# Five transformed pairs instead of four in each quarter of the down projection, with sums of weights brought in by transfers into the residual's room

## The chip, the cores and the metric

The kernel runs on one core of one Trainium2 chip. The metric is the time of one execution on the device, in microseconds (us), as the median of several runs. Engines go by the profile's names: PE is the matrix engine (PEld its weight loads), DVE the vector engine, ACT the scalar engine, POOL and SP the two engines whose queues issue transfers here. Each engine works through its own instructions strictly in the program's order.

## The reference

One layer of a decoder trunk on 256 tokens of width D = 2048, in fp32: a block of attention in two branches, then a channel mixer, then a gated embedding. The change lies in the channel mixer and in what keeps the residual `h` from it to the end:

```python
    h = h + rmsnorm(mix, g_mix_post[i])
    u = rmsnorm(h, g_ffn_pre[i])
    up = causal_depthwise_conv(u @ w_up[i], conv_w[i], conv_b[i])
    gate_ff, value = jnp.split(up, [D_FF], axis=-1)
    f = (jax.nn.gelu(gate_ff, approximate=True) * value) @ w_down[i]
    h = h + rmsnorm(f, g_ffn_post[i])
    e = p[i] @ w_ple_in[i]
    h = h + jax.nn.sigmoid((h @ w_ple_gate[i]).astype(jnp.float32)).astype(h.dtype) * e
```

D_FF is 5632, so `w_up` has 2 x 44 columns of tiles of 128 and `w_down` 44 rows of tiles.

## The kernel before

**Weights in two parts.** All weights lie packed in DRAM in the order in which PE uses them. An item is eight 128x128 blocks, one 128x1024 tile of 512 KB. `load` (L199) brings an item into one of 5 raw tiles (NRAW), `high` (L228) lets ACT write its rounded high part `hi`, and `low` (L291) lets DVE write the remainder `lo` = raw - hi (L301). There are 7 pairs of hi and lo tiles (NSPL). A product is three matmuls, high times high, low times high, high times low (`three_wide`, L943, matmuls on L945; in `up`, `mul` with L382 and L384).

**What sets the order.** The order is written out by hand through `tick` (L326), which runs each time PE begins a new item: it lets ACT write high parts up to six items ahead of PE (`reach`, L220), lets DVE write the low parts of all items up to five ahead, and then runs the deferred work that is due (`defer`, `due`). `lows` (L317) also emits the load of an item as soon as a raw tile is released in the program's order, on SP's queue. So DVE's queue holds, at each tick, first the low parts for items that PE will need later, and then the deferred vector work.

**Quarters.** The channel mixer runs in four quarters, q = 0 to 3 (loop at L1382): 22 column groups of `up` (16 blocks each), whose evacuation (`up_evac`, L1211) leaves 11 rows of tiles in `ft`, then `down` for these 11 rows. `down` of a quarter has three parts: a group of output columns 0 to 1023 (`strassen`, L1253), and two groups of 512 columns, `plain(2)` and `plain(3)` (L1393, `four`). In q = 0 `plain(2)` comes ahead of `strassen`, in the other quarters directly behind it.

**Pairs.** In `strassen`, rows go in pairs (DROWS = 8, four pairs) and the last three rows singly (`plains`, 12 matmuls each). A pair takes seven products, 21 matmuls of 512 columns, where two single rows take 24. For that it needs sums of activations, which `parts` (L1193) makes during `up` into the tile `mixed` (four subtractions, one copy by ACT, one subtraction), and sums of weights. A pair is four items of the stream: the first raw item, two items of sums, and half an item. The sums are `raw` tiles of their own (`weight_sums`, L240): for most pairs DVE makes them, four additions of 128x512 (L254, L255, L257, L258); for the first two pairs of each quarter (DSUM) the first two additions are left to transfers: `sum_early` (L280) loads the first raw item a second time into a tile `tsum` and adds half of the second item to it twice through POOL's queue (`accum_op=OP.add`, L277), so that DVE makes two (L257, L258). The two tiles of `tsum` are one of their own and two borrowed from the tag `t`.

**Banks.** Results lie in 8 PSUM banks handed out by `bank` (L415). `strassen` uses all eight: products 1, 5, 6, 7 and the four output tiles. In q > 0 `plain(2)` needs two banks again while DVE still has the outputs to put together: ACT copies product 1 away (L1279), and DVE's `join_to` (L1307) begins with `x2 = product 6 + copy of product 1` (L1311), seven more instructions (L1312 to L1318) follow, and `ends` (L1320) adds the four output tiles. The first bank of `plain(2)` is released by the copy of product 1; the second one is the bank of product 6, and is released by L1311. `join_to` is deferred: it stands in DVE's queue behind the low parts that the tick of the first single row emits. In q = 0 `join_first` (L1298) reads product 6, and the group that waits for its bank is `plain(3)`.

**The residual.** `home` (L1243) writes the residual, 16 KB a partition, into the tile `hx` early in `up`; it lies there unused until `apply` (L1443) adds the normalized output of `down` to it. Before, its room holds the first half of `e` for a moment (`turn`, L1105), which is written to DRAM and read back later (`e0`).

## Time and profile before

| | |
|---|---|
| median of 3 runs | 1434.43 us (1434.07 to 1434.95) |
| the profiled execution | 1434.18 us; its span, first to last instruction, is 1432.0 us |
| granted PE clock, mean | 0.999 |
| ACT busy | 860.0 us, 60% of the span |
| transfers on SP's queue | 285.76 MB, 59.6% of the time of 16 DMA engines |
| transfers on POOL's queue | 11.54 MB, 4.7% |

Rows of groups give the busy time and the mean duration of one instruction; rows of the timeline give start, duration, engine, line, operation and operands, and in brackets how long the engine was idle before and what ended that. Instructions overlap a little: one starts before the record of the one ahead ends, so the distance from start to start is what an instruction costs in a full queue. The chain of waits goes from the last instruction back to the first, at each step to what released it.

### The profile page before, as it was taken

What the parts mean: (1) busy time and instruction counts of PE and PEld (TensorE: products, weight loads), DVE (VectorE), ACT (ScalarE), POOL (GpSimd) and SP (SyncE); (2) the same over time, 40 slices, a digit from 0 to 9 for tenths busy, and PEclk for the clock granted to TensorE, in tenths of its full rate; (3) what the DMA queues carried; (4) which work ended last, traced back from release to release, by engine and by line L of the source; (5) the groups of instructions that cost most, each with busy time, mean ns of one, the idle gap of its engine ahead of it and who ended that gap; (6) DMA issues with size and microseconds to landing.
All of it is one profiled execution on the core that took longest, in us unless ns stands there. A gap on an engine that the chain in (4) does not pass through costs nothing.

```text
span 1432.0 us, 20556 instructions
## 1 busy us (share of the span) xinstructions
PE 1423.4 (99%) x7511; PEld 1222.8 (85%) x7511; DVE 1167.4 (82%) x1791; ACT 860.0 (60%) x1296; POOL 39.4 (3%) x49
## 2 busy tenths in 40 slices
PE   9999999999999999999999999999999999999998
PEld 8888888888888888998888888888888888888787
DVE  7876666669889965779999788987889878899797
ACT  7665555566555655576665666655665555657464
POOL 0000000002110000000000000000000000000000
PEclk9999999999999999999999999999999999999999
DMA  7754746479985766547657865377653776538654
GB/s 290 268 168 160 245 141 219 148 240 255 298 230 200 268 216 218 185 162 226 203 170 245 256 196 177 118 277 235 206 179 114 272 233 207 183 112 303 181 176 162
DMA packets 87908, 298.60 MB, mean 209 GB/s; under 512 B 9728, under 2 KB 10368, under 8 KB 87552
## 3 DMA queue, kind: packets, MB, share of 16 engines
q1 hardware_dynamic: 81472, 285.76, 59.6%
q0 software_dynamic: 6336, 11.54, 4.7%
q8 instruction: 59, 0.97, 0.3%
q14 instruction: 41, 0.34, 0.1%
HBM read 294.11 MB, written 3.15 MB: 208 GB/s over the span
## 4 chain that ended last, share of the span: by engine, by line
PE 93%; DVE 6%; ACT 1%; issue 0%; ACTq 0%; DVEq 0%
PE mm L382 32%; PE mm L945 27%; PE mm L384 16%; PE mm L708 2%; PE mm L710 2%; PE mm L709 2%; PE mm L863 2%; PE mm L864 2%; PE mm L865 2%; DVE lo L295 2%; DVE lo L301 1%; PE S L382 0%; DVE wsum L257 0%; PE mm L404 0%; PE mm L403 0%; PE mm L402 0%
## 5 line engine op out<-in xcount | busy, mean ns | idle before, releaser
L301 DVE TENSOR_TENSOR lo<-raw,hi 128x1024 fp32r<-128x1024 f32 (+1 forms) x498 | 582.0, 1186 | 105.6 <-ACT hi L238 100.7
L382 PE MATMUL mm<-u,hi 128*128 128x512 f32 x1804 | 627.4, 392 | 0.0
L238 ACT ACTIVATE hi<-raw 128x1024 fp32r<-128x1024 f32 (+1 forms) x498 | 504.5, 1027 | 175.6 <-PE mm L382 54.2
L384 PE MATMUL mm<-u,lo 128*128 128x256 f32 x1791 | 501.4, 280 | 0.0
L382 PEld LDWEIGHTS mm<-u,hi 128*128 128x128 f32 x1804 | 336.7, 187 | 72.4
L384 PEld LDWEIGHTS mm<-u,lo 128*128 128x128 f32 x1791 | 338.5, 189 | 0.7
L945 PE MATMUL mm<-hi,ft 128*128 128x512 f32 x544 | 173.8, 390 | 0.9 <-ACT hi L234 0.9
L945 PE MATMUL mm<-hi,u 128*128 128x512 f32 (+1 forms) x464 | 148.0, 389 | 0.6 <-DVE u L1486 0.5
L440 ACT ACTIVATE t<-mm 128x256 f32<-128x256 f32 x131 | 49.8, 380 | 149.1 <-PE mm L384 149.1
L945 PEld LDWEIGHTS mm<-hi,ft 128*128 128x128 f32 x544 | 102.1, 188 | 22.9 <-ACT hi L234 2.2
L945 PE MATMUL mm<-lo,ft 128*128 128x512 f32 x272 | 106.3, 391 | 0.7 <-DVE lo L295 0.7
L945 PEld LDWEIGHTS mm<-hi,u 128*128 128x128 f32 x464 | 86.4, 188 | 19.1 <-DVE u L1486 2.1
L443 DVE TENSOR_TENSOR s<-mm,t 128x256 f32<-128x256 f32 x116 | 49.0, 423 | 54.1 <-ACT t L440 54.0
L945 PE MATMUL mm<-lo,u 128*128 128x512 f32 (+1 forms) x232 | 89.6, 386 | 0.0
L382 PE MATMUL mm<-mg,hi 128*128 128x512 f32 x232 | 80.5, 392 | 0.0
L234 ACT ACTIVATE hi<-wsum 128x512 fp32r<-128x512 f32 x84 | 50.7, 629 | 49.1 <-DVE wsum L257 40.2
L384 PE MATMUL mm<-mg,lo 128*128 128x256 f32 x230 | 64.4, 280 | 0.0
L945 PEld LDWEIGHTS mm<-lo,ft 128*128 128x128 f32 x272 | 51.0, 188 | 12.6 <-DVE lo L295 2.0
L1222 ACT ACTIVATE cv<-cpad,cw 128x256 f32<-128x256 f32 x88 | 52.6, 598 | 12.1 <-DVE cpad L1217 12.0
L945 PE MATMUL mm<-hi,mixed 128*128 128x512 f32 x160 | 55.8, 390 | 0.0
L295 DVE TENSOR_TENSOR lo<-wsum,hi 128x512 fp32r<-128x512 f32 x84 | 54.6, 688 | 1.3 <-ACT hi L234 0.7
L945 PEld LDWEIGHTS mm<-lo,u 128*128 128x128 f32 x232 | 43.6, 188 | 9.0 <-DVE lo L295 0.5
(327 smaller groups left out, 1837.8 us busy)
## 6 DMA issues: line engine op xcount, KB each, us to landing
raw<-in_w SPq DMA_DIRECT2D x478, 512.0 KB, 4.0
gh<-in_w SPq DMA_DIRECT2D x12, 512.0 KB, 5.9
gh<-in_w POOLq DMA_DIRECT2D x24, 256.0 KB, 7.8
raw<-in_w SPq DMA_DIRECT2D x24, 256.0 KB, 3.4
tsum<-in_w POOLq DMA_DIRECT2D x20, 256.0 KB, 7.0
hd<-in_head SPq DMA_DIRECT2D x6, 576.0 KB, 7.4
gh<-in_gx SPq DMA_DIRECT2D x6, 512.0 KB, 4.5
tsum<-in_w SPq DMA_DIRECT2D x5, 512.0 KB, 4.5
```

The lines of the kernel that those rows point to most:

```text
L234: ACT.activation(hi[i][:, n * 512:(n + 1) * 512], x, AF.Copy)
L238: ACT.activation(hi[i][:, a:b], raw[i][:, a:b] if src is None else src, AF.Copy)
L295: DVE.tensor_tensor(lo[i][:, to], x, f(hi[i][:, to]), OP.subtract)
L301: DVE.tensor_tensor(lo[i][:, a:b], raw[i][:, a:b] if src is None else src, f(hi[i][:, a:b]), OP.subtract)
L382: PE.matmul(ps, wh, rhs, start=first, stop=last, skip_group_check=True)
L384: PE.matmul(ps[:, :T], wl, rhs[:, :T], start=False, stop=last, skip_group_check=True)
L440: ACT.activation(t1[0], ps[:, T:], AF.Copy)
L443: DVE.tensor_tensor(out, ps[:, :T], t1[0], OP.add)
L708: PE.matmul(pv[t], xh, wh, start=kt == 0, stop=False)
L709: PE.matmul(pv[t], xh, wl, start=False, stop=False)
L945: PE.matmul(ps, x[i], w[j], start=first and n == 0, stop=last and n == 2, skip_group_check=True)
L1222: ACT.activation(y, c[:, 2:], AF.Identity, scale=cw[:, n, 2:3], bias=cw[:, n, 3:4])
```

## The change

DROWS becomes 10, so `strassen` has five pairs and one single row in each quarter. All five pairs get their first sums by transfers. Their places are `tsum`, the two tiles of tag `t`, and three of the four 4 KB-wide pieces into which `hx` is cut (tags hx1 to hx3); the fourth piece (hx0) holds the transformed activations of the fifth pair. To free this room the residual is written to DRAM (`h1`, 2 MB, four transfers) after `home` has made it, and read back by four transfers in the last quarter, behind the single row of `strassen`. `e0` is written in two transfers instead of one, and `finish` makes two additions of 512 columns where it made one of 1024. The pairs of the last stage (`pg`) keep what they had.

```diff
-DROWS = 8
-DSUM = 2
+DROWS = 10
+DSUM = {"down": DROWS // 2, "pg": 2}
...
-                if g[0][0] == "pairs" and p < DSUM:
+                if g[0][0] == "pairs" and p < DSUM[g[0][1]]:
                     early_sums.append(i)
...
         i = early_sums.pop(0)
-        if n == 0:
-            sum_to(i, mps["mp"].tile([128, 1024], F32, name="tsum", tag="tsum"))
+        if n != 1:
+            sum_to(i, mps["mp"].tile([128, 1024], F32, name="tsum", tag=f"hx{n - 1}" if n else "tsum"))
             return
...
-    hx = fp.tile([128, 2, D], F32, name="hx")
+    def residual():
+        return [fp.tile([128, 2, 512], F32, name="hx", tag=f"hx{n}") for n in range(4)]
+
+    hx = residual()
...
-    nc.sync.dma_start(e0, hx[:, :, :D // 2])
+    h1 = dram.tile([128, 2, D], F32, name="h1")
+    for n in range(2):
+        nc.sync.dma_start(e0[:, :, n * 512:(n + 1) * 512], hx[n])
...
+    def mixing(ps):
+        x = keep.tile([128, PAIRS, 2, 4, H], F32R, name="mixed", tag="gh")
+        for p in range(ps):
+            mixed[p] = x[:, p] if p < PAIRS else fp.tile([128, 2, 4, H], F32R, name="mixed4", tag="hx0")
...
     sp = halves()
-    mixed = keep.tile([128, PAIRS, 2, 4, H], F32R, name="mixed", tag="gh")
+    for n in range(4):
+        nc.sync.dma_start(h1[:, :, n * 512:(n + 1) * 512], hx[n])
+    mixing(DROWS // 2)
...
+    AHEAD = (0, 1, 4, 7, 10)[:DROWS // 2]
     for q in range(NQ):
...
             at_n = n - max(len(pss), q * 2 * QT) - 2
-            0 <= at_n < DSUM and sum_early(at_n)
+            at_n in AHEAD and sum_early(AHEAD.index(at_n))
...
         next(s)
         defer((None, lambda bk=bk, o=o: ends(o, bk)))
         if end:
+            hx = residual()
+            for n in range(4):
+                nc.sync.dma_start(hx[n], h1[:, :, n * 512:(n + 1) * 512])
             squared(range(2))
...
             DVE.tensor_tensor(o, o, ee[:, t, a:b], OP.mult)
-            DVE.tensor_tensor(o, o, hx[:, t, a:b], OP.add)
+            for c in range(a, b, 512):
+                x = min(b - c, 512)
+                to = ff[:, t, c:c + x]
+                DVE.tensor_tensor(to, to, hx[c // 512][:, t, c % 512:c % 512 + x], OP.add)
             nc.sync.dma_start(out[:, t, a:b], o)
```

The changed lines stand ten to twenty lines lower in the changed kernel: `join_to` begins at L1321 instead of L1311, `join_first` is L1308.

DVE in q = 1, from the last pair to the `join`. Before, the last pair of four: four additions of weights, the low parts of its four items, then the low parts of the three single rows and of the first three items of `plain(2)`, then L1311:

```order
L254 TENSOR_TENSOR wsum<-raw 128x512
L255 TENSOR_TENSOR wsum<-raw 128x512
L301 TENSOR_TENSOR lo<-raw,hi 128x1024
L295 TENSOR_TENSOR lo<-wsum,hi 128x512 x2
L257 TENSOR_TENSOR wsum<-wsum,raw 128x512
L258 TENSOR_TENSOR wsum<-wsum,raw 128x512
L295 TENSOR_TENSOR lo<-wsum,hi 128x512 x2
L301 TENSOR_TENSOR lo<-raw,hi 128x512
L301 TENSOR_TENSOR lo<-raw,hi 128x1024 x6
L1311 TENSOR_TENSOR x_9171<-mm,x_8950 128x512
L1312 TENSOR_TENSOR ff<-ff,x_8950 128x512
```

The same place in the changed kernel, the last pair of five:

```order
L301 TENSOR_TENSOR lo<-raw,hi 128x1024
L257 TENSOR_TENSOR wsum<-tsum,raw 128x512
L258 TENSOR_TENSOR wsum<-wsum,raw 128x512
L295 TENSOR_TENSOR lo<-tsum,hi 128x512 x2
L295 TENSOR_TENSOR lo<-wsum,hi 128x512 x2
L301 TENSOR_TENSOR lo<-raw,hi 128x512
L301 TENSOR_TENSOR lo<-raw,hi 128x1024 x6
L1321 TENSOR_TENSOR x_9271<-mm,x_9006 128x512
L1322 TENSOR_TENSOR ff<-ff,x_9006 128x512
```

L254 and L255 are gone from the pair. Six low parts still stand between it and the join; they are now those of one single row and of the first five items of `plain(2)`.

PE in q = 1, the end of `strassen` and the beginning of `plain(2)`, with the engines each waits for. Before, the last two matmuls of the third single row and the first four of `plain(2)`:

```order
L945 MATMUL mm<-lo,ft 128x512
L945 MATMUL mm<-hi,ft 128x512
L945 MATMUL mm<-hi,ft 128x512 [waits Activation_49]
L945 MATMUL mm<-lo,ft 128x512 [waits DVE_49]
L945 MATMUL mm<-hi,ft 128x512
L945 MATMUL mm<-hi,ft 128x512 [waits DVE_49]
```

In the changed kernel, the last matmuls of the only single row and the first four of `plain(2)`:

```order
L945 MATMUL mm<-lo,ft 128x512
L945 MATMUL mm<-hi,ft 128x512
L945 MATMUL mm<-hi,ft 128x512 [waits PE_49]
L945 MATMUL mm<-lo,ft 128x512
L945 MATMUL mm<-hi,ft 128x512
L945 MATMUL mm<-hi,ft 128x512 [waits Activation_49]
L945 MATMUL mm<-lo,ft 128x512 [waits DVE_49]
L945 MATMUL mm<-hi,ft 128x512
L945 MATMUL mm<-hi,ft 128x512 [waits DVE_49]
```

The fourth matmul of `plain(2)` writes into the bank of product 6 and waits for the join's first instruction on DVE, in both kernels; from the last matmul of a pair to it there are now 15 matmuls, where there were 39.

SP at the end of q = 3, the changed kernel, where the residual is read back (`h_5990` is the copy in DRAM, `g_12834` the gains, `e_5989` the stored half of `e`):

```order
L204 DMA raw<-in_w 128x1024 x10
L1437 DMA g_12834<-in_gains 128x2048
L204 DMA raw<-in_w 128x1024
L1444 DMA hx<-h_5990 128x2x512 x4
L204 DMA raw<-in_w 128x1024 x11
L1484 DMA ee<-e_5989 128x2x1024
```

Before, the fourth row was not there and 14 loads of weights stood between the gains and the stored half of `e`.

## The prediction

> **What bounds the kernel now.** The page comes first, its busy times and the chain that ended last:

> ```profile
> PE 1423.4 (99%) x7511; PEld 1222.8 (85%) x7511; DVE 1167.4 (82%) x1791; ACT 860.0 (60%) x1296; POOL 39.4 (3%) x49
> PE 93%; DVE 6%; ACT 1%; issue 0%; ACTq 0%; DVEq 0%
> ```

> PE is the bound almost everywhere; the 6% of the chain that are DVE's lie in few places. So I looked for them in the chain in order of time. In q = 1 it leaves PE at 905 us and comes back at 929 us (the third and the fourth pair):

> ```profile
> 915.76 0.60 DVE wsum L254
> 916.37 0.60 DVE wsum L255
> 916.97 1.14 DVE lo L301
> 918.10 1.20 DVE lo L295 x2
> 919.31 0.61 DVE wsum L257
> ...
> 922.63 0.60 DVE wsum L254
> ...
> 928.95 40.22 PE mm L945 x176
> ```

> Two things are read here. A pair whose sums DVE makes takes DVE 922.63 - 915.76 = 6.87 us. And a matmul of this form takes PE 40.22 / 176 = 0.2285 us, so the 21 of a pair take 4.80 us: inside `strassen` DVE is the slower engine and uses up a lead that it won during `up`. PE's timeline shows what that costs at the fourth pair:

> ```profile
> 928.22 0.50 PE L945 MATMUL mm<-hi,ft 128*128 128x512 f32 x1 [0.29 <-ACT hi L234]
> 928.95 0.50 PE L945 MATMUL mm<-lo,ft 128*128 128x512 f32 x1 [0.23 <-DVE lo L295]
> ...
> 939.54 0.62 PE L945 MATMUL mm<-hi,ft 128*128 128x512 f32 x2
> ```

> The brackets understate it, since the record of a matmul (0.39 us) is longer than its distance to the next. From the one that started 0.68 us ahead of 928.22 to 928.95 lie two distances of 0.2285 us too many: the loss is 0.95 us a quarter (q = 1 to 3, about 2.85 us in all). The row at 939.54 holds the third and the fourth matmul of `plain(2)`; the fourth starts at 939.54 + 0.2285 = 939.77, and it is the one that waits for the join's first instruction. How near was that? DVE's timeline from the last low part of the fourth pair on, and ACT's for the load:

> ```profile
> 928.81 0.69 DVE L301 TENSOR_TENSOR lo<-raw,hi 128x512 fp32r<-128x512 f32 x1
> 929.67 5.91 DVE L301 TENSOR_TENSOR lo<-raw,hi 128x1024 fp32r<-128x1024 f32 x5 [0.18 <-ACT hi L238]
> 937.46 1.23 DVE L301 TENSOR_TENSOR lo<-raw,hi 128x1024 fp32r<-128x1024 f32 x1 [1.88 <-ACT hi L238]
> 938.60 0.69 DVE L1311 TENSOR_TENSOR x<-mm,x 128x512 f32<-128x512 f32 x1
> ...
> 936.37 1.06 ACT L238 ACTIVATE hi<-raw 128x1024 fp32r<-128x1024 f32 x1 [2.04 <-DMA raw<-in_w]
> ```

> L1311 ends at 939.29, **0.48 us ahead** of the matmul that needs it. It stands behind six low parts, and the sixth waits for a load that could be issued only when the first of the six had freed a raw tile. From the end of the pair (929.50) to the end of L1311 are 9.8 us. In the other quarters the same pair of rows (DVE's L1311 and PE's third and fourth matmul), for q = 2, then q = 3:

> ```profile
> 1118.11 0.69 DVE L1311 TENSOR_TENSOR x<-mm,x 128x512 f32<-128x512 f32 x1
> 1119.98 0.61 PE L945 MATMUL mm<-hi,ft 128*128 128x512 f32 x2
> 1299.00 0.68 DVE L1311 TENSOR_TENSOR x<-mm,x 128x512 f32<-128x512 f32 x1
> 1300.41 0.61 PE L945 MATMUL mm<-hi,ft 128*128 128x512 f32 x2
> ```

> There the slack is 1120.21 - 1118.80 = 1.41 and 1300.64 - 1299.68 = 0.96 us. That is all the room the change has at this place.

> **The change part by part.** *PE's work.* A fifth pair saves 24 - 21 = 3 matmuls, 0.69 us a quarter, 2.74 us in four. If nothing else stood in the way, the 0.95 us of waiting at the fourth pair would go too, and `plain(2)` would reach its fourth matmul 0.95 + 0.69 = 1.64 us sooner: at 938.13 in q = 1, 1118.57 in q = 2, 1299.00 in q = 3.

> *DVE's work ahead of the join.* A pair whose sums come by transfer costs DVE no L254 and L255, and what it costs is seen in the rows of the second pair in q = 1:

> ```profile
> 905.81 0.42 DVE L443 TENSOR_TENSOR s<-mm,t 128x256 f32<-128x256 f32 x1 [1.05 <-ACT t L440]
> ...
> 908.82 0.68 DVE L257 TENSOR_TENSOR wsum<-tsum,raw 128x512 f32<-128x512 f32 x1
> 909.53 0.69 DVE L258 TENSOR_TENSOR wsum<-wsum,raw 128x512 f32<-128x512 f32 x1
> 910.15 1.28 DVE L295 TENSOR_TENSOR lo<-tsum,hi 128x512 fp32r<-128x512 f32 x2
> ...
> L1199 DVE TENSOR_TENSOR y<-cv,cv x16: 283/286/291, 662.8 to 1243.9; 128x128 f32<-128x128 f32 x16
> ```

> From start to start: L257 0.71, L258 0.62; and as in the chain's rows the first item 1.14, two low parts 1.20, two more 1.20, half an item 0.61 like any 128x512 operation there; together 5.5 us. The third and the fourth pair thus become 6.87 - 5.5 = 1.37 us shorter each, and a fifth of 5.5 us is added. Its activations add four subtractions of 0.28 us (last row), which fit into the 1.05 us that DVE stands idle ahead of 905.81, where they come in the order, and one subtraction of 128x512 (0.60 us), behind which DVE has no idle time until 929. DVE comes to the end of the last pair later by 5.5 - 2.74 + 0.6 = **3.4 us** (3.2 if L254's 0.60 and L255's 0.61 alone had to go and the rest ran tighter, 4.5 if the four subtractions found no room). Behind it stand again six low parts of 1.14 us and the same load, issued when the first of the six is done, so the stretch to L1321 (before: L1311) stays as measured.

> *The new wait.* L1321 ends at 939.29 + 3.4 = 942.7, 1122.2 and 1303.1 us, and PE starts 0.06 us later (928.89, the end of the low part, to 928.95 above). PE is there at 938.13, 1118.57 and 1299.00: **it waits 4.6, 3.7 and 4.2 us**. Against before the fourth matmul of `plain(2)` starts later by 942.75 - 939.77 = 3.0, by 2.05 and by 2.5 us, 7.55 in all. Behind it in PE's queue lies everything that is left; PE works without a pause to the next quarter, so nothing gives it back. The wait swallows both gains in these three quarters.

> *q = 0.* Here `plain(2)` comes first, DVE starts `strassen` with its full lead, and the join's first instruction is L1298:

> ```profile
> 769.84 0.69 DVE L1298 TENSOR_TENSOR ff<-mm,ff 128x512 f32<-128x512 f32 x1
> 774.02 0.62 PE L945 MATMUL mm<-hi,ft 128*128 128x512 f32 x2
> ```

> Slack 774.25 - 770.53 = 3.72 us. DVE comes 5.5 - 2.74 = 2.76 us later, PE 0.69 us sooner, and 0.27 us are left: gain 0.69, with 0.6 more on DVE a wait of 0.3.

> *Transfers.* Three more pairs a quarter load 0.5 MB more each and add 2 x 256 KB, the residual goes out (2 MB) and comes back (2 MB).

> ```profile
> raw<-in_w SPq DMA_DIRECT2D x478, 512.0 KB, 4.0
> tsum<-in_w POOLq DMA_DIRECT2D x20, 256.0 KB, 7.0
> e<-hx SPq DMA_DIRECT2D x1, 1024.0 KB, 6.3
> ee<-e SPq DMA_DIRECT2D x1, 1024.0 KB, 7.5
> ```

> The last sums are asked for nine groups of `up` before the pairs, some 50 us (16 x 0.348 = 5.57 us a group, from the rows of `up` in PE's timeline), and take 4 + 2 x 7 = 18: no cost; without that cover DVE waits at L257. The writes take SP's queue about 13 us at 6.3 us a MB. Queued behind them on SP are loads of `up`, of which five raw tiles at 2.8 us are in hand, 14 us: no cost, at worst a few us. The reads stand on SP behind loads up to the item that the join waits behind, not ahead of it; `apply` needs them at the end of `plain(3)`, some 30 us on, and they take 4 x 4 to 2 x 7.5 us. Loads of `plain(2)` queue behind them, with ten items of 2.74 us (five raw tiles, five pairs of hi and lo) in hand. Two more additions in `finish` lie under the last group's matmuls. All taken as zero; bounds 0 to +4 us together.

> *The sum*, on the profiled execution: 1434.18 + 7.55 - 0.69 = 1441.04; that execution was 0.25 us under the median of the runs, which is nothing here. I say **1441.0 us**, 0.47% slower.

> [...] In the window from 927 to 930, with 0.95 us lost, the granted clock was full:

> ```profile
> 927.00:930.00 3.00, 2.49 (x11) 1.49 (x10) 2.76 (x5) 2.99 (x5) 0.00 (x0) 1.00 0.53 178
> ```

> No stall of before lasts longer, so its trace can't tell what one of 4 us does. [...]

> **The rivals.** (1) *Faster:* the join is in time and PE stays the bound. Then both gains stand: 1434.18 - 2.74 - 2.85 = 1428.6. For it speaks that PE is 99% busy; against it that DVE would have to reach L1321 some 4 us sooner than its rows add up to. It decides at 938.1 us in q = 1. (2) *No change:* the join is late, but the sixth low part no longer waits for its load, because raw tiles are released more evenly. Its idle time was 1.88 us in q = 1, and from the 9.8, 8.8 and 9.3 us to the end of L1311 against six times 1.14 and 0.69 and a gap of 0.2, some 4 us fall away in three quarters: 1441.0 - 4.1 = 1436.9, and with a few tenths less on DVE 1436. Against it: the sixth load is still issued behind the first low part. (3) *Slower still by the clock:* if PE came back from each wait at half speed for as long as the wait was, it would lose half of 4.6 + 3.7 + 4.2, 6.2 us: 1447. (4) *Slower still by transfers:* loads late behind the writes or the reads, up to 4 us: 1445. (5) *It does not do what it says:* sums late, DVE waiting at L257; POOL's 18 us against 50 speak against it; 1445 or more.

> **How the numbers follow.** Forecast 65%, (1) 7%, (2) 13%, (3) 8%, (4) 5%, (5) 2%. The range leaves out (1), most of (3) and (5), and reaches from 1434.5 (case 2 with the short ends on DVE) to 1446 (the 1.1 us of four uncovered subtractions in three quarters, or case 4). 0.2% is about what a measurement of this kernel can tell from no change; 1436.9 lies just within it. Faster 7%, same 13%, slower 80%.

> **What would show it.** Right: in q = 1 to 3 PE idle once for about 4 us, a few matmuls into `plain(2)`, released by DVE's L1321; no idle at L945 inside the pairs; L254 and L255 gone from `down`; the chain on DVE from the end of `up` through six L301 to L1321; in q = 0 at most 0.3 us. Wrong: no such idle time (rival 1), a sixth low part that follows the fifth at once (2), a granted clock under 1.00 behind the wait (3), idle time of ACT at loads, or of DVE at L257 (4, 5).

## The result, and the profile after

The changed kernel takes 1446.03 us (median of 5 runs, 1445.48 to 1447.59) against 1434.83 us: a ratio of 1.0081, 95% interval 1.0069 to 1.0094. It is slower, as forecast, but by 11.2 us where 6.6 were forecast, just outside the range. The profiled execution took 1445.48 us (before 1434.18), its span is 1443.7 us.

The page of the changed kernel, busy times, the chain by engine, and the group of matmuls ahead of which PE now stands idle; the last row is the same group before:

```profile
PE 1425.2 (99%) x7499; PEld 1224.1 (85%) x7499; DVE 1175.1 (81%) x1821; ACT 867.1 (60%) x1316; POOL 60.5 (4%) x73
PE 92%; DVE 5%; issue 1%; DMA 1%; ACT 1%; ACTq 0%
L945 PE MATMUL mm<-hi,ft 128*128 128x512 f32 x504 | 167.1, 398 | 11.2 <-DVE x L1321 11.2
...
L945 PE MATMUL mm<-hi,ft 128*128 128x512 f32 x544 | 173.8, 390 | 0.9 <-ACT hi L234 0.9
```

PE is "99% busy" as before, so the share tells nothing. The first row has something odd, though: PE has 12 matmuls fewer, 2.74 us of work, and yet 1.8 us more busy time. And one matmul of the group took 390 ns on the mean before and takes 398 ns now. The waits of PE (total, times, longest) have one new entry, the first row; the two entries of the fourth pair, the rows of before below it, are gone:

```profile
PE mm L945 <- DVE x L1321: 11.2, 3, 4.2
...
PE mm L945 <- ACT hi L234: 0.9, 3, 0.3
PE mm L945 <- DVE lo L295: 0.7, 3, 0.2
```

Where each lies is seen in PE's timeline in q = 1:

```profile
937.24 0.39 PE L945 MATMUL mm<-hi,ft 128*128 128x512 f32 x1
941.83 0.50 PE L945 MATMUL mm<-hi,ft 128*128 128x512 f32 x1 [4.21 <-DVE x L1321]
942.17 0.43 PE L945 MATMUL mm<-lo,ft 128*128 128x512 f32 x1
942.40 1.05 PE L945 MATMUL mm<-hi,ft 128*128 128x512 f32 x2
943.25 0.63 PE L945 MATMUL mm<-lo,ft 128*128 128x512 f32 x1
...
945.81 0.40 PE L945 MATMUL mm<-lo,ft 128*128 128x512 f32 x1
946.05 0.63 PE L945 MATMUL mm<-hi,ft 128*128 128x512 f32 x2
```

The third matmul of `plain(2)` starts at 937.24, the fourth at 941.83: 4.59 - 0.23 = 4.36 us of waiting. From 942.40 to 945.81 the distance from matmul to matmul is not 0.2285 but 0.43 us. The windows of that place, each 3.41 us long (columns: length, busy time and count of PE, PEld, DVE, ACT, POOL, then the granted clock, the DMA share and GB/s), and below them the slow one of q = 2 and that of q = 3:

```profile
935.57:938.98 3.41, 2.05 (x10) 1.36 (x8) 2.86 (x3) 1.18 (x2) 0.00 (x0) 1.00 0.95 315
938.98:942.40 3.42, 0.57 (x2) 0.48 (x3) 2.42 (x3) 3.04 (x3) 0.00 (x0) 1.00 1.03 407
942.40:945.81 3.41, 3.41 (x9) 2.64 (x8) 3.33 (x6) 0.20 (x2) 0.00 (x0) 0.50 0.53 203
945.81:949.22 3.41, 3.41 (x16) 2.81 (x15) 3.41 (x6) 1.54 (x2) 0.00 (x0) 1.00 0.20 42
...
1126.72:1130.13 3.41, 3.41 (x9) 2.65 (x9) 3.34 (x6) 0.83 (x2) 0.00 (x0) 0.50 0.57 225
1311.04:1314.45 3.41, 3.41 (x10) 2.64 (x9) 3.34 (x6) 0.77 (x1) 0.00 (x0) 0.50 1.03 426
```

Behind each wait the granted clock is 0.50 for one stretch of 3.41 us, in which PE makes 9 or 10 matmuls instead of 16. From the distances of the matmuls, 1.71, 1.71 and 1.69 us are lost there, 5.1 in all. A matmul at half clock counts as busy; hence the odd first row.

How much each quarter costs is read from an instruction that both kernels have behind it, here the first evacuation of `up` (L440) in q = 1, 2 and 3, ahead of the arrow before and behind it after: 794.40 -> 793.70, 974.88 -> 978.71, 1155.32 -> 1162.85; and PE's last matmul, 1426.74 -> 1438.27. The rows of q = 2, before and after:

```profile
974.88 0.39 ACT L440 ACTIVATE t<-mm 128x256 f32<-128x256 f32 x1 [1.86 <-PE mm L384]
...
978.71 0.39 ACT L440 ACTIVATE t<-mm 128x256 f32<-128x256 f32 x1 [1.86 <-PE mm L384]
```

The first row of the table is the first of these differences; each further row is what the next difference adds to it:

| us | forecast | measured | of it the clock | without the clock |
|---|---|---|---|---|
| q = 0 | -0.69 | -0.70 | 0 | -0.70 |
| q = 1 | +3.0 | +4.53 | 1.71 | +2.82 |
| q = 2 | +2.05 | +3.70 | 1.71 | +1.99 |
| q = 3 and on | +2.5 | +4.00 | 1.69 | +2.31 |
| sum | +6.86 | +11.53 | 5.11 | +6.42 |

The chain in q = 1, in order of time, shows why the join is late:

```profile
933.82 4.93 DMA raw<-in_w
938.86 1.06 ACT hi L238
939.95 1.22 DVE lo L301
941.17 0.61 DVE x L1321
941.83 31.17 PE mm L945 x129
```

It is the sixth low part: its load runs from 933.82 on, when the first of the six low parts has freed a raw tile, then ACT's high part, the low part, the join's first instruction, PE.

### The profile page after: what moved, and what is told of

It reads as the page before. It is cut to its first block, busy times and chain, and to the rows that moved or that the text cites. A ratio compares the mean times of both kernels' runs of the same rounds, so it can differ in the third digit from the quotient of the medians.

```text
span 1443.7 us, 20693 instructions
## 1 busy us (share of the span) xinstructions
PE 1425.2 (99%) x7499; PEld 1224.1 (85%) x7499; DVE 1175.1 (81%) x1821; ACT 867.1 (60%) x1316; POOL 60.5 (4%) x73
## 4 chain that ended last, share of the span: by engine, by line
PE 92%; DVE 5%; issue 1%; DMA 1%; ACT 1%; ACTq 0%
PE mm L382 32%; PE mm L945 24%; PE mm L384 17%; PE mm L710 2%; PE mm L708 2%; PE mm L709 2%; PE mm L865 2%; PE mm L864 2%; PE mm L863 2%; DVE lo L295 2%; DVE lo L301 2%; DMA raw<-in_w 1%; PE S L382 0%; ACT hi L238 0%; DVE wsum L257 0%
## 5 line engine op out<-in xcount | busy, mean ns | idle before, releaser
L301 DVE TENSOR_TENSOR lo<-raw,hi 128x1024 fp32r<-128x1024 f32 (+1 forms) x498 | 579.3, 1180 | 109.8 <-ACT hi L238 105.0
L238 ACT ACTIVATE hi<-raw 128x1024 fp32r<-128x1024 f32 (+1 forms) x498 | 501.7, 1022 | 183.1 <-PE mm L945 55.2
L945 PE MATMUL mm<-hi,ft 128*128 128x512 f32 x504 | 167.1, 398 | 11.2 <-DVE x L1321 11.2
L945 PE MATMUL mm<-hi,u 128*128 128x512 f32 (+1 forms) x464 | 147.9, 389 | 0.6 <-DVE u L1503 0.5
L440 ACT ACTIVATE t<-mm 128x256 f32<-128x256 f32 x131 | 49.7, 380 | 149.2 <-PE mm L384 149.2
L945 PEld LDWEIGHTS mm<-hi,ft 128*128 128x128 f32 x504 | 96.7, 192 | 33.2 <-DVE x L1321 12.5
L945 PEld LDWEIGHTS mm<-hi,u 128*128 128x128 f32 x464 | 86.4, 188 | 19.1 <-DVE u L1503 2.2
L945 PE MATMUL mm<-lo,ft 128*128 128x512 f32 x252 | 100.2, 397 | 0.0
L443 DVE TENSOR_TENSOR s<-mm,t 128x256 f32<-128x256 f32 x116 | 49.0, 422 | 51.6 <-ACT t L440 51.5
L945 PE MATMUL mm<-lo,u 128*128 128x512 f32 (+1 forms) x232 | 89.6, 386 | 0.0
L277 POOL DMA_DIRECT2D tsum<-in_w x44 | 38.8, 1022 | 895.9 <-DMA tsum<-in_w 547.3
L234 ACT ACTIVATE hi<-wsum 128x512 fp32r<-128x512 f32 x76 | 46.3, 629 | 42.4 <-DVE wsum L257 33.4
L945 PE MATMUL mm<-hi,mixed 128*128 128x512 f32 x192 | 66.9, 389 | 0.0
L945 PEld LDWEIGHTS mm<-lo,ft 128*128 128x128 f32 x252 | 48.6, 193 | 11.1 <-DVE lo L295 1.1
L945 PEld LDWEIGHTS mm<-lo,u 128*128 128x128 f32 x232 | 43.6, 188 | 9.1 <-DVE lo L295 0.5
## 6 DMA issues: line engine op xcount, KB each, us to landing
raw<-in_w SPq DMA_DIRECT2D x466, 512.0 KB, 4.3
tsum<-in_w POOLq DMA_DIRECT2D x44, 256.0 KB, 7.3
raw<-in_w SPq DMA_DIRECT2D x36, 256.0 KB, 2.9
tsum<-in_w SPq DMA_DIRECT2D x17, 512.0 KB, 4.8
gh<-in_w SPq DMA_DIRECT2D x12, 512.0 KB, 4.5
gh<-in_w POOLq DMA_DIRECT2D x24, 256.0 KB, 7.1
gh<-in_gx SPq DMA_DIRECT2D x6, 512.0 KB, 4.5
```

The costliest lines, as they stand in the source:

```text
L234: ACT.activation(hi[i][:, n * 512:(n + 1) * 512], x, AF.Copy)
L238: ACT.activation(hi[i][:, a:b], raw[i][:, a:b] if src is None else src, AF.Copy)
L277: nc.gpsimd.dma_start(x, w[stream[i] + 1 - NE][:, 512:], accum_op=OP.add)
L301: DVE.tensor_tensor(lo[i][:, a:b], raw[i][:, a:b] if src is None else src, f(hi[i][:, a:b]), OP.subtract)
L440: ACT.activation(t1[0], ps[:, T:], AF.Copy)
L443: DVE.tensor_tensor(out, ps[:, :T], t1[0], OP.add)
```

## The experiments

Two questions were put: is it only the place of one instruction on DVE that costs time, and what decides whether the clock falls?

**The join's first instruction behind two low parts instead of six** (the changed kernel otherwise). The low parts are held back for the last pair, and the instruction is written directly behind it:

```diff
-            lows(max(before, min(i + 2, at["high"])))
+            lows(min(at["cap"], max(before, min(i + 2, at["high"]))))
...
+            if last and cap:
+                at["cap"] = at["block"] // 8 + 4 + 2
...
+            x2 = tmp.tile([128, 512], F32, name="x2", tag="s2", bufs=2)
+            DVE.tensor_tensor(x2, bk[6], x, OP.add)
+            at["cap"] = NI
```

> The changed kernel, but in q = 1 to 3 the join's first instruction stands behind two of the six low parts instead of six. Theory (the wait for the bank of product 6 and what follows it on PE is all of the loss): the instruction ends near 935.5 us in q = 1, two us ahead of the matmul that needs it; no wait at L945, granted clock 1.00 throughout; 1445.5 less the waits of 4.4, 3.5 and 3.8 us and less three times 1.7 us at half clock: near 1429 us. Rival (transfers or the sums hold the kernel up): the loss shows at another place, and the time stays over 1434.

Measured: 1428.45 us (4 runs), ratio to before 0.9962 (0.9947 to 0.9977). DVE's timeline in q = 1 (this execution is 1.5 us behind the changed kernel's when q = 1 begins, by L440 at 795.21 against 793.70):

```profile
933.47 2.96 DVE L301 TENSOR_TENSOR lo<-raw,hi 128x512 fp32r<-128x512 f32 x3
936.35 0.68 DVE L1437 TENSOR_TENSOR x<-mm,x 128x512 f32<-128x512 f32 x1
936.95 1.22 DVE L301 TENSOR_TENSOR lo<-raw,hi 128x1024 fp32r<-128x1024 f32 x1
```

The instruction (here L1437) ends at 937.03, and PE has no wait at L945 for it in any quarter; the clock's mean is 0.999. The theory holds: one instruction's place is worth some 17 us, and behind it both gains of the change are there. This is the best version found; it beats both kernels.

**Four pairs, all by transfers, residual in DRAM**: `DROWS = 8`, the rest as changed.

> The changed kernel with four pairs a quarter instead of five, all four with their first sums by transfers, the residual still in DRAM. Theory: DVE comes to the join 2.7 us sooner than before and PE has its 39 matmuls, so there is no wait; what goes against before is the 0.95 us at the fourth pair, three times, less about 0.2 that stays: 1431.5 to 1432.5. Rival (the added transfers, the residual's write and read cost time of their own): 1434.5 or more.

Measured: 1430.07 us (7 runs), ratio 0.9971 (0.9959 to 0.9982). A little better than expected, in part because the wait at the fourth pair is gone altogether: no wait of PE at L945 in the pairs is left, where the expectation let 0.2 us stay. In the two traces the same evacuations as above put the kernel with the moved join 1.6 us ahead of before in each of q = 1 to 3, this one 1.1 us; the fifth pair itself is worth the difference, about 0.45 us a quarter. The intervals of the two ratios overlap.

**The residual alone**: written and read back, four pairs, two of them by transfers (`DROWS = 8`, `DSUM = {"down": 2, "pg": 2}`).

> The kernel before with the residual written to DRAM and read back, four pairs, sums as before. Theory (the traffic costs nothing): within 0.5 us of before. Rival (writes or reads make loads late): 2 to 4 us slower.

Measured: 1434.77 us (10 runs), ratio 0.9999 (0.9990 to 1.0009). The 4 MB of traffic cost nothing that can be measured.

**The join moved in the kernel before**, as in the first experiment.

> The kernel before, with the join's first instruction behind two low parts instead of six, as in the first kernel. Theory: there was no wait to remove, so no change: 1434.4, and the 0.95 us at the fourth pair remains in q = 1 to 3. Rival (the move is worth something by itself and the fifth pair little): 1431 or less.

Measured: 1434.76 us (10 runs), ratio 0.9999 (0.9990 to 1.0009). Its waits are still those of before:

```profile
PE mm L945 <- ACT hi L234: 0.9, 3, 0.3
PE mm L945 <- DVE lo L295: 0.7, 3, 0.2
```

So the move gains nothing by itself; it only lets the pairs have their gain.

**The fifth pair without transfers**: the changed kernel with `DSUM = {"down": 2, "pg": 2}` (and the list `AHEAD` shortened to match), so that DVE makes the sums of the third to fifth pair.

> The changed kernel, but only the first two pairs of a quarter have their first sums by transfers as before; the third to fifth pair's are made by DVE. By the rows of before DVE comes 3 x 1.37 = 4.1 us later to the join than in the changed kernel. Theory (PE waits for DVE, and loses about 1.7 us more behind a wait of over 3 us whatever its length): 12.3 us more in q = 1 to 3, in q = 0 some 4 us of new waiting and 1.7 us: near 1464 us. Rival (half clock for as long as the wait): 2 us more for each, near 1470. Rival (the transfers of the sums are what costs in the changed kernel): below 1446.

Measured: 1462.69 us (one run), against some 1464 expected. That the sum comes out so near is in part luck. A part of the waiting has moved into the pairs (at L301, L234 and L295, 7.4 us together), with 3.9 us the longest wait for L1321. In q = 0 the wait was only 1.6 us and the clock stayed at 1.00, so the 1.7 us expected there for the clock are missing; in q = 1 two stretches in a row were slow (949.04 to 955.87), 1.2 us more than expected. With the join where it is, the transfers are needed for a fifth pair; they are not what costs.

**The join behind five low parts**, so that only the sixth and its load are behind it (`+ 4 + 5` in place of `+ 4 + 2`).

> As the first kernel, but the join's first instruction stands behind five low parts, so that it no longer waits for the sixth one and its load: it ends some 2.5 us sooner than in the changed kernel, and the waits of PE become about 1.9, 1.0 and 1.3 us. Theory that the clock falls only behind a long wait: 1445.5 - 7.4 - 5.1 = 1433.0, clock 1.00. Rival that it falls behind each wait for its length: 1445.5 - 7.4 - 5.1 + 2.1 = 1435.1. Rival that it falls there whatever the wait: 1438.1.

Measured: 1434.34 us (10 runs), ratio 1.0000 (0.9991 to 1.0010). PE's waits and the windows around the first of them:

```profile
PE mm L945 <- DVE x L1437: 4.7, 3, 1.7
...
936.00:939.41 3.41, 2.03 (x9) 1.34 (x8) 3.31 (x4) 1.23 (x2) 0.00 (x0) 1.00 0.93 286
939.41:942.80 3.39, 3.25 (x14) 2.72 (x15) 2.51 (x4) 2.93 (x3) 0.00 (x0) 1.00 1.01 402
```

From start to start the waits are 1.67, 1.82 and 1.69 us, and the clock stays at 1.00 behind all three: it does not fall behind each wait. The expected 1433.0 was 1.3 us too low; 1.0 of it is that the waits are 5.2 us in all instead of the 4.2 worked out.

**The kernel before, with six additions on DVE ahead of its join**, which write a tile that the join then overwrites:

```diff
+        for _ in range(6):
+            tt(x2, x, x, OP.add)
         tt(x2, bk[6], x, OP.add)
```

> The kernel before, with six additions of 128x512 on DVE that change no result ahead of the join's first instruction (0.6 to 0.72 us each, 3.6 to 4.3 us). Waits at L945 in q = 1 to 3 of some 3.1 to 3.8, 2.2 to 2.9 and 2.6 to 3.4 us. Theory (half clock only behind a wait over some length between 0.95 and 3.5 us, and then 1.7 us lost): 1434.2 + 8 to 10 = 1442 to 1444, plus 1.7 for each wait over that length. Rival (half clock for as long as the wait was): half of the waits on top, 4 to 5 us, in all three places.

Measured: 1449.29 us (one run). The waits are 3.14, 2.93 and 3.10 us; 1.71, 1.67 and 1.40 us are lost behind them, so the half clock comes in the kernel before too. About 1 us more is lost in this execution before the quarters begin, where PE waits 0.7 us for `gb` (L878); no other trace has that wait. The third place tells most (PE's timeline, then the windows):

```profile
1311.24 0.39 PE L945 MATMUL mm<-hi,ft 128*128 128x512 f32 x1
1314.58 0.79 PE L945 MATMUL mm<-hi,ft 128*128 128x512 f32 x1 [2.94 <-DVE x L1313]
...
1310.60:1314.01 3.41, 1.03 (x5) 0.53 (x3) 3.17 (x6) 2.30 (x4) 0.00 (x0) 1.00 1.02 419
1314.01:1317.43 3.42, 2.85 (x7) 2.27 (x8) 3.32 (x6) 0.77 (x1) 0.00 (x0) 0.50 0.44 181
1317.43:1320.84 3.41, 3.41 (x17) 2.80 (x16) 3.41 (x5) 0.00 (x0) 0.00 (x0) 1.00 0.00 0
```

Here the clock fell at 1314.01, 0.57 us ahead of PE's return, so less work fell into the slow stretch, and less was lost.

**The same with five additions.**

> The kernel before with five additions of 0.7 us on DVE ahead of the join's first instruction: waits of about 2.4, 2.2 and 2.4 us, between those of 1.7 to 1.8 us that left the clock at 1.00 and those of 2.9 us and more that halved it. Theory (the clock is set for stretches of 3.41 us on a fixed grid by how busy PE was in the stretch before, with the border somewhere between 35% and 48% busy): which of the waits are followed by half a clock depends on how they lie on the grid, so runs differ by up to 1.7 us for each; 1441 us without any, 1446 with all three. Rival (the length of the wait alone decides): each run the same, all or none.

Measured: 1446.94 us (4 runs: 1447.21, 1446.82, 1447.06, 1444.79). Waits in the profiled execution 2.46, 2.62 and 2.37 us, each followed by half a clock; the windows of the third:

```profile
1308.67:1312.08 3.41, 1.29 (x6) 0.75 (x4) 3.20 (x6) 2.34 (x3) 0.00 (x0) 1.00 1.00 404
1312.08:1315.50 3.42, 3.33 (x8) 2.69 (x9) 3.32 (x7) 1.06 (x1) 0.00 (x0) 0.50 0.61 254
```

So a stretch in which PE is busy for 1.29 of 3.41 us (38%) was followed by half a clock. That the grid, and not the length alone, decides is only half answered: the run of 1444.79 has a mean clock of 0.997 against 0.995 and 0.996 in the others, as with one slow stretch fewer, but only one of the four runs left a trace.

**The wait filled**: the changed kernel, PE makes the first product of `plain(2)` five times more while it waits.

```diff
+                    for _ in range(again if (k, t) == (0, 0) else 0):
+                        three_wide(ps[t], cut(src, k, t), got[k], True)
                     three_wide(ps[t], cut(src, k, t), got[k], k == 0)
```

> The changed kernel, but PE makes the first product of plain(2) five times over in q = 1 to 3 (15 more matmuls of 0.2285 us, 3.43 us), while it would wait for L1321; the repeats start the sum anew, so nothing changes in the result. Theory (a third to a half of the loss is the clock that falls because PE stands idle): the instructions end where they did, the waits shrink to about 0.9, 0.1 and 0.4 us, the clock stays at 1.00, and the three times 1.7 us go: 5.1 us less than the changed kernel, near 1441. Rival (half clock comes with the place, not with the idleness): as the changed kernel, 1446. Rival (PE had a use for that time): 1446 and more.

> The changed kernel itself, on the same chip as the one with the wait filled: 1445.5 to 1447.6 as measured, with half a clock behind each of three waits.

Measured on one chip: 1441.86 us filled (4 runs; ratio to before 1.0049, 1.0034 to 1.0064), 1446.22 us not filled (4 runs; 1.0078, 1.0061 to 1.0095). Windows of 10 us around the three places, filled:

```profile
936.00:946.00 10.00, 9.45 (x42) 7.51 (x41) 8.64 (x11) 5.41 (x6) 0.00 (x0) 1.00 0.94 348
1121.00:1131.00 10.00, 10.00 (x46) 8.29 (x45) 9.66 (x13) 5.73 (x6) 0.00 (x0) 1.00 0.70 276
1305.00:1315.00 10.00, 9.61 (x43) 7.64 (x42) 9.46 (x14) 4.95 (x6) 0.00 (x0) 1.00 0.97 361
```

PE does 45 matmuls that nobody needs, the clock stays at 1.00, and the kernel is 4.4 us faster. The join is about as late as in the changed kernel; what is gone is the price of standing idle. By the evacuations and the last matmul as above, q = 1 to 3 cost 2.6, 1.9 and 2.6 us against before in this kernel, near the last column of the table (2.8, 2.0 and 2.3), which was worked out in another way. Together with the table above: of the 11.5 us, some 6.4 are the later join, less the gains, and some 5 the clock.

## Why the prediction was wrong

- *The bound and the place.* Right: PE idle once in each of q = 1 to 3, at the fourth matmul of `plain(2)`, released by L1321, and at no other place in these quarters for more than the 0.2 us told below. Moving that one instruction (the first experiment) gave 1428.45 us; rival (1), which let the join be in time, was worked out as 1428.6.
- *The gains.* Right in size: q = 0 gave 0.70 (forecast 0.69). The 0.95 us at the last pair did not go altogether in the changed kernel: two distances of 0.33 us, from 931.78 to 932.45, leave about 0.2 us in q = 1, and the same in q = 2 and 3.
- *DVE's delay and the waits.* Near: forecast 4.6, 3.7 and 4.2 us, measured 4.36, 3.50 and 3.80. Two errors nearly cancel here. DVE was 3.9 us late at the end of the last pair, not 3.4 (in q = 1, 932.66 against 929.49, and the 0.70 by which the quarter began sooner); and the stretch from there to the end of L1321, which was to stay as measured, took 9.1, 8.3 and 8.5 us where it had taken 9.8, 8.8 and 9.3. The absolute times were 0.7 us too late, since the gain of q = 0 was not carried into the later quarters; for the waits that makes no difference. The load of the sixth low part stayed on the path as forecast, and rival (2) did not come, though that shorter stretch is a part of what it named. By its own terms (9.8, 8.8 and 9.3 us, each less six times 1.14, 0.69 and 0.2) it would have taken off 4.7 us, not 4.1, and the top of the range is not what its reason gives: three times 1.1 us on 1441.0 is 1444.3.
- *Transfers.* Right at zero: the residual alone changes nothing, and PE waits for no load.
- *The step that failed* is the price of the waits. They were priced at full clock, and half a clock, which the trace of before shows only at its end, where PE has no work left (0.50 from 1430 to 1432), was left to rival (3) with 8%. The row from which the full clock was taken (1.00 in the window from 927 to 930) shows 0.95 us of loss in 3 us, and the text said itself that it can't tell what a wait of 4 us does; so it was no evidence for full clock, and yet the sum has no term for the clock. The runs show in its place 1.71, 1.71 and 1.69 us lost at half clock behind the three waits, 5.1 us in all. In q = 1 the stretch ahead of the slow one has PE busy for 0.57 of 3.42 us. Rival (3) was right in kind: the granted clock behind the three waits was 0.50. Its price was not: half of each wait, 6.2 us, where the runs show one stretch of 3.41 us for most waits, whatever their length: 1.71 us behind 4.36 and behind 3.51 us, and 1.7 us behind 2.46 (five additions, q = 1) and behind 4.10 (the fifth pair without transfers, q = 3). The exceptions stand at the end.

Forecast and clock together, 1441.04 + 5.1 = 1446.1 us, are the measured median. That they fall on it exactly is luck: in the profiled execution, 1445.48 us, the part without the clock was 6.4 us and not the forecast 6.9.

## What to carry to other kernels

The waits of the matrix engine had up to two prices here: their length, and a slow stretch behind them (4.36 and 1.71 us in q = 1 of the changed kernel). In the traces waits of 2.4 us and more had both, and waits of up to 1.8 us only the first; so a long wait can be worth filling even where it can't be removed (4.4 us less here). When work is shortened on the engine that is the bound, look for the instruction of another engine that releases its buffers, and for what stands ahead of that instruction in its queue: here one addition of 0.6 us behind two instead of six low parts turned a loss of 11 us into a gain of 6. And a busy share doesn't show any of this, since slow work counts as busy (3.41 of 3.41 us with 9 matmuls instead of 16); the granted clock in short windows does (0.50 there).

## What the runs showed of the hardware

```profile
1117.33:1120.75 3.42, 1.76 (x9) 1.14 (x8) 3.18 (x4) 2.15 (x3) 0.00 (x0) 1.00 1.02 376
```

Whether a border in busy time lies between these two, no run set out to measure.

In two runs a slow stretch was followed by another. In the repeat of the changed kernel PE came back 0.7 us into a stretch at half clock (940.94), and the next one was slow as well:

```profile
936.85:940.27 3.42, 1.20 (x6) 0.66 (x4) 3.21 (x4) 2.00 (x2) 0.00 (x0) 1.00 1.01 386
940.27:943.68 3.41, 2.74 (x7) 2.19 (x8) 3.31 (x7) 2.11 (x2) 0.00 (x0) 0.50 1.00 407
943.68:947.10 3.42, 3.42 (x10) 2.68 (x9) 3.42 (x5) 1.06 (x1) 0.00 (x0) 0.50 0.08 31
947.10:950.51 3.41, 3.41 (x16) 2.81 (x15) 3.41 (x6) 1.07 (x1) 0.00 (x0) 1.00 0.53 159
```

A stretch at half clock with 2.74 us busy was followed by another slow one, and so was one with 2.72 us in the fifth pair without transfers (q = 1):

```profile
949.04:952.45 3.41, 2.72 (x6) 2.15 (x7) 3.31 (x7) 1.99 (x2) 0.00 (x0) 0.50 1.03 420
952.45:955.87 3.42, 3.42 (x9) 2.64 (x8) 3.42 (x5) 1.06 (x1) 0.00 (x0) 0.50 0.23 93
```

One with 2.85 us (the third place with six additions) was followed by full clock. In the repeat that wait of 3.05 us cost 2.99 us behind it, more than waits of 4 us elsewhere. It would explain why the runs of the changed kernel spread over 2.1 us (1445.48 to 1447.59) with mean clocks of 0.995 and 0.994, where those of before spread over 0.9; that is read from single traces and not shown.
